# A hybrid decoder layer on one core: 45 matrix passes moved ahead of the first attention score, and a smaller allowance per attention step

## The chip, the core and the metric

The kernel runs on one core of one Trainium2 chip. The core has a matrix engine (TensorE, PE in the rows, with its weight loads as PEld), a vector engine (VectorE, DVE), an activation engine (ScalarE, ACT), a general engine (GpSimd, POOL) and a queue engine that only issues transfers (SyncE, SP). Each engine works through its own list of instructions in order and waits on semaphores for the others. Sixteen DMA engines move data between the core's memory and the chip's main memory; most transfers are issued by SP, some by ACT. The metric is the device time of one execution in microseconds, as the median of three runs.

## The reference

One decoder layer over 1024 tokens of width 1024, in float32:

- a root-mean-square norm and one projection of 3592 columns, split between two groups of heads;
- group one: four heads of a gated delta rule, with short convolutions on q, k and v, in chunks, and a gated norm;
- group two: four heads of differential attention. A head has two query/key maps of 64 columns. Each map gives causal scores with a relative-position bias and a softmax; the second map, times a learned lambda, is taken from the first, and the result is multiplied with the values and normed;
- the outputs of both groups side by side through one output projection, added to the input;
- a norm, a gated feed-forward layer of 2816 columns, added, and a last norm.

The lines of the reference that the change lies on:

```
s = jnp.einsum('bqhmd,bkhmd->bhmqk', q_blk, k).astype(jnp.float32)
s = s + bias.transpose(2, 0, 1)[None, :, None]
s = jnp.where(rel >= 0, s, -jnp.inf)
p = jax.nn.softmax(s, axis=-1)
p = p[:, :, 0] - lam * p[:, :, 1]
return jnp.einsum('bhqk,bkhe->bqhe', p.astype(v.dtype), v)
```

## The kernel before, in words

Dense products are computed to float32 accuracy from operands split into a high and a low part: `mm3` (lines 143 to 146) issues three passes, high by high, high by low and low by high. A **pass** below is one such matmul instruction with 512 moving columns.

The program runs in this order: norm and transposition of the input (`xT_h`, `xT_l`); values of all attention heads; the delta-rule heads; queries and keys of attention heads 0 and 1; then the **attention part**, into which other matrix work is woven; then the feed-forward layer.

The attention part has 32 **steps** k (list `steps`): four heads, eight blocks of 128 queries each, blocks 0 to 7 for heads 0 to 2 and 7 to 0 for head 3. Block i sees i+1 blocks of keys. A step's work is spread over the loop: `emit_S(k)` computes the scores of both maps, adds the bias, takes the maximum (DVE) and the exponential (ACT); `emit_P(k)` forms the difference of the two maps (DVE, line 931); `emit_T(k-1)` transposes the step before (line 946); `emit_PV(k-2)` multiplies the one before that with the values (line 961).

The other matrix work, the **filler**, is the generator `fill` (line 785). In this order it yields: queries of head 2 (48 passes, called Q2 below), keys of head 2 (K2), Q3, K3, with the gating of a delta-rule head (`finish_gate`) between or inside them; four empty yields (`SKIP`); 16 units of 12 passes of the output projection's first half (tiles named `fl<-w_h,av`); a wait until blocks 7 to 4 of head 3 are through; and 8 more units of 12 passes. In K2 the gating of head 0 stands between the first 24 passes and the last 24 (the call `mid()`): it transposes into the two `fl` buffers that the passes also use, and DVE (line 745) reads them together with a tile `cv<-sz` that SP loads. That load needs a buffer that holds Q2 until Q2 has been written to main memory.

`pump(n)` takes n passes from the filler; what a call takes too much is owed by the next. `share(k)` sets n for a step by the block number i: 22 - 5i/2, of which 5 come after the transposes, 4 between two groups of transposes in long steps, and the rest before; where that rest is negative it is nothing, so a long step gets 9. Over a head these are 22, 19.5, 17, 14.5, 12, 9.5, 9 and 9 passes. With them, K3's last pass falls into step 12 and the output projection's last into step 29.

SP's list is kept in the order of the program (`manual_schedule`). The other engines' lists are ordered by a scheduler that goes by its own durations. `load_head(h)` (line 698) loads a head's queries, keys (`ak<-ks`) and bias, `load_v` its values; both are called at steps 4, 12 and 20 for the next head, and before the loop for head 0. The keys of a head are written to main memory by ACT's queue (lines 604 and 605) and loaded again from there. After K3, `fetch_o` loads quarters of the output weights (`w_raw<-in_w_out`) into the space that K3's operands leave, and `take_o` splits them (ACT line 151, then DVE line 153 or POOL line 157). Each unit adds to a residual tile `xh` (SP line 775, DVE line 770).

Of the kernel before, what the change touches and what calls it, by code (L numbers as in the profile page):

```python
# [31 lines left out]
SQRT_MAX = 1.8446743e19  # L32
LAM_CAP = 1e12
SKIP = 4
LAM_INIT = 0.8 - 0.6


# [31 lines left out]
def decoder_kernel(ctx: ExitStack, tc: tile.TileContext, a: dict, out: bass.AP):  # L69
# [100 lines left out]
    def cvt(dtype=F32):  # L170
        return cv.tile([P, T], dtype, name="cv", bufs=4)
# [75 lines left out]
    nc.sync.dma_start(out=dnw, in_=a["diff_norm_w"][0].rearrange("(p o) -> p o", o=1))  # L247
    nc.vector.tensor_scalar(out=dnw, in0=dnw, scalar1=1.0 - LAM_INIT, scalar2=None, op0=ALU.mult)

    ab = const.tile([P, NT, 8], F32, name="ab")  # L250
    for half in range(2):
        n = 264 if half == 0 else 256
# [47 lines left out]
    for i, nm in enumerate(("lambda_q1", "lambda_k1", "lambda_q2", "lambda_k2")):  # L300
# [8 lines left out]
    nlam, mag, kap, nlc, epsi, thr = (lc[:, i:i + 1] for i in range(6))  # L309
    nc.vector.scalar_tensor_tensor(out=nlam, in0=ls[:, 1:2], scalar=-LAM_INIT, in1=ls[:, 0:1],  # L310
                                   op0=ALU.add, op1=ALU.subtract)
# [86 lines left out]
    def fetch(key, src, shape, which=0):  # L398
        pool, bufs = wpools[which]
        raw = pool.tile(shape, F32, name="w_raw", bufs=bufs)  # L400
        nc.sync.dma_start(out=raw, in_=src)
        raws[key] = pool, raw, shape
# [5 lines left out]
    def qk_col(h, is_q):  # L408
        c = (C_QD if is_q else C_KD) + h * P
        return w_in_v[:, :, c:c + P], [P, NK, P]  # L410
# [221 lines left out]
    for j in range(NT):  # L632
# [38 lines left out]
        for h in range(H):  # L671
            ps = pss[h]
            i = h * 8 + j
# [25 lines left out]
    def load_head(h):  # L699
        load_q(h, first_half(h))  # L700
        kt = ap_.tile([P, 2, T], F32R, name="ak", bufs=2)
        nc.sync.dma_start(out=kt.bitcast(F32), in_=ks_dr[h].rearrange("(m d) t -> d m t", m=2))
        kk = [kt[:, m, :] for m in range(2)]
        bias = ap_.tile([P, 256], F32, name="bias", bufs=2)
        nc.sync.dma_start(out=bias, in_=bias2_dr[:, h, :])
        head[h] = kk, bias

    def first_half(h):
        return 1 if h == H - 1 else 0
# [4 lines left out]
    def load_q(h, half):  # L714
        hc = slice(half * 512, (half + 1) * 512)
        parts = []
        for nm, src in (("aqh", qh_dr[h]), ("aql", ql_dr[h])):
            qt = ap_.tile([P, 2, 512], F32R, name=nm, bufs=2)
            for o in range(2):
                nc.sync.dma_start(out=qt[o * DH:(o + 1) * DH].bitcast(F32),  # L720
                                  in_=src[:, hc].rearrange("(m d) t -> d m t", m=2))
            parts.append(qt)
        queries[h, half] = parts

    def load_v(h):
        vals[h] = ap_.tile([P, NT, P], F32, name="avd", bufs=2)
        nc.sync.dma_start(out=vals[h], in_=vd_dr[h])
# [29 lines left out]
    def fetch_o(group, u, i):  # L757
        us = slice(u * 512, (u + 1) * 512)
        fetch((group, u, i), wo_v[:, 4 * group + 2 * i:4 * group + 2 * i + 2, us], [P, 2, 512], i)
# [24 lines left out]
    def fill():  # L784
# [25 lines left out]
        fetch_o(1, 0, 1)  # L810
        for _ in range(SKIP):
            yield -1
# [39 lines left out]
    def load_mix_d(half, n):  # L852
        for h in range(n):
            hc = slice(half * 512, (half + 1) * 512)
            m = late["mix"][half][h]
            raw = m[:, 512:1024].bitcast(F32)
            nc.sync.dma_start(out=raw, in_=md[h][:, hc])
            nc.scalar.copy(out=m[:, 0:512], in_=raw)
            nc.gpsimd.tensor_tensor(out=m[:, 512:1024], in0=raw, in1=m[:, 0:512].bitcast(F32), op=ALU.subtract)
# [3 lines left out]
    def share(k):  # L863
        i = steps[k][1] if k < len(steps) else 0
        prev = steps[k - 1][1] if 0 < k <= len(steps) else 0
        n = 22 - 5 * i / 2
        pb = 4 if prev >= 4 else 0
        return max(0, n - pb - 5), pb, 5

# [3 lines left out]
    def pump(n):  # L873
        nonlocal credit
        credit += n
        while credit > 0:
            c = next(filler, -1)
            if c < 0:
                credit = 0
                return  # L880
            credit -= c
# [53 lines left out]
    def emit_T(k, gap):  # L935
        h, i = steps[k]
        pp, rz = st[k]
        pt = ap_.tile([P, T], F32, name="apt", bufs=2)
        for b in range((i + 4) // 4):
            if b:  # L940
                pump(gap)
            ps = sma()
            nblk = min(4, i + 1 - 4 * b)
            for kk in range(nblk):
                kb = 4 * b + kk
                nc.tensor.transpose(ps[:, kk * P:(kk + 1) * P], pp[:, kb * P:(kb + 1) * P], ident)
            nc.scalar.copy(out=pt[:, b * 512:b * 512 + nblk * P], in_=ps[:, :nblk * P])
        st[k] = pt, rz
# [3 lines left out]
    def emit_PV(k):  # L952
        h, i = steps[k]
        pt, rz = st.pop(k)
        vd = vals[h]
        if k % 4 == 0:
            osum[h] = sma(), ap_.tile([P, 512], F32, name="aon", bufs=2)
        O, on = osum[h]
        oc = slice((i % 4) * P, (i % 4 + 1) * P)
        for kb in range(i + 1):  # L960
            nc.tensor.matmul(O[:, oc], lhsT=pt[:, kb * P:(kb + 1) * P], rhs=vd[:, kb, :],  # L961
                             start=(kb == 0), stop=(kb == i))
        nc.scalar.activation(out=on[:, oc], in_=O[:, oc], func=AF.Copy, scale=rz[:, 0:1])
        if k % 4 != 3:
            return
        nc.scalar.activation(out=O, in_=on, func=AF.Square)
        ms = small.tile([P, 4], F32, name="ams", bufs=3)
        nc.vector.tensor_reduce(out=ms, in_=O.rearrange("p (a b) -> p a b", a=4), axis=AX.X, op=ALU.add)
        ok = small.tile([P, 4], F32, name="aok", bufs=3)
        nc.vector.tensor_scalar(out=ok, in0=ms, scalar1=thr, scalar2=None, op0=ALU.is_lt)  # L970
        nc.vector.tensor_scalar(out=ms, in0=ms, scalar1=1.0 / DV, scalar2=epsi, op0=ALU.mult, op1=ALU.add)
        nc.vector.tensor_scalar(out=ms, in0=ms, scalar1=1e-37, scalar2=None, op0=ALU.max)
        nc.gpsimd.tensor_tensor(out=ms, in0=ms, in1=epow_neg[:, 0:4], op=ALU.pow)
        nc.vector.tensor_tensor(out=ms, in0=ms, in1=ok, op=ALU.mult)
        onv = on.rearrange("p (a b) -> p a b", a=4)
        nc.vector.tensor_tensor(out=onv, in0=onv,
                                in1=ms.rearrange("p (a o) -> p a o", o=1).broadcast_to([P, 4, P]), op=ALU.mult)
        osum["on"] = on
# [22 lines left out]
    with tc.manual_schedule(engines={mybir.EngineType.SP}):  # L1001
        fetch((2, True), *qk_col(2, True))
        fetch((2, False), *qk_col(2, False))
        load_head(0)
        load_v(0)
        for k in range(len(steps) + 4):

            def values():
                if 2 <= k < len(steps) + 2:
                    emit_PV(k - 2)  # L1010

            if k < len(steps):
                emit_S(k, values)
                if k % NT == 0:
                    load_q(k // NT, 1 - first_half(k // NT))
                if k % NT == 4 and k // NT + 1 < H:
                    load_head(k // NT + 1)
                    load_v(k // NT + 1)
            else:
                values()  # L1020
            if k == 28:
                late["mix"][1] = [cvt(F32R) for h in range(H)]
                load_mix_d(1, H - 1)
            pa, pb, pc = share(k)
            pump(pa)
            if 1 <= k <= len(steps):
                emit_T(k - 1, pb)
            pump(pc)
            if k > 2 and (k - 3) % 4 == 3:
                emit_OT(k - 3)  # L1030
            if k < len(steps):
                emit_P(k)
            if k == len(steps):
                while 0 not in late["mix"]:
                    pump(12)
                load_mix_d(0, H - 1)
        while "d1" in late:
            c = next(filler, None)
            if c is None:
                break  # L1040
# [369 lines left out]
```

## Time and profile before

| | |
|---|---|
| median of 3 runs | 1378.44 us (1376.91 to 1378.69) |
| the profiled execution | 1377.38 us |
| its span, first to last instruction | 1375.5 us |
| mean granted share of TensorE's clock | 0.988 |
| attention part in that span | about 406 to 657 us |
| PE busy, share of the span | 95% |
| DVE, ACT, POOL busy | 56%, 36%, 19% |

The span is divided into stages that bind differently, so shares over the whole span say little about one stage. Times in the rows are counted from the first instruction. Matmuls are pipelined: one pass is shown as 0.39 us long, while passes that follow each other start 0.23 us apart. Idle time of an engine stands in square brackets with what ended it.

### The profile page before, as it was taken

To read this page: it belongs to the slowest core of one execution; us is meant where nothing else is said; L and a number is where in the kernel's file an instruction comes from. 1 tells how busy PE (TensorE), PEld (TensorE's weight loads), DVE (VectorE), ACT (ScalarE), POOL (GpSimd) and SP (SyncE) were. 2 spreads that over 40 slices of the span, in tenths; PEclk is the share of its full clock that TensorE was granted. 3 is DMA by queue.
4 is the path that set the end of the run, shared out by engine and by line. 5 is a ranking of instruction groups with operands and counts; after the bars stand their busy time and mean duration, and the time that the engine had idled before them with its cause. 6 is when DMAs were issued, how large, how long until landed. Compare 5 with 4: busy or idle time off the path is not lost.

```text
span 1375.5 us, 17042 instructions
## 1 busy us (share of the span) xinstructions
PE 1305.1 (95%) x6540; PEld 1086.2 (79%) x6540; DVE 768.1 (56%) x1282; ACT 497.1 (36%) x948; POOL 262.5 (19%) x211
## 2 busy tenths in 40 slices
PE   6999999899988998998889999999999999999997
PEld 6968888798967777887667877787878788788886
DVE  6516649625833675876884555455545536545325
ACT  5233321233733654553543333232323235112104
POOL 1010052100042331113332121211121214200003
PEclk9999999999998999999999999999999999999999
DMA  7321113101055655734432233222222248422003
GB/s 216 110 62 47 31 44 97 29 1 47 1 145 182 208 179 185 237 119 168 145 100 77 94 100 98 79 75 92 92 77 73 80 134 280 152 92 92 0 1 123
DMA packets 122425, 143.31 MB, mean 104 GB/s; under 512 B 13632, under 2 KB 90728, under 8 KB 122344
## 3 DMA queue, kind: packets, MB, share of 16 engines
q1 hardware_dynamic: 114432, 128.07, 30.0%
q10 hardware_dynamic: 7912, 14.16, 2.8%
q8 instruction: 51, 0.84, 0.3%
q14 instruction: 30, 0.25, 0.1%
HBM read 103.40 MB, written 38.80 MB: 103 GB/s over the span
## 4 chain that ended last, share of the span: by engine, by line
PE 70%; DVE 13%; DMA 5%; issue 4%; ACT 4%; POOL 3%; SPq 1%; POOLq 0%; DVEq 0%; ACTq 0%
PE big L1177 17%; PE sm L1177 8%; PE fl L144 4%; PE fl L145 4%; PE fl L146 4%; PE fl L1177 4%; PE big L144 3%; PE big L145 3%; PE big L146 3%; PE sm L144 3%; PE sm L146 3%; PE sm L145 3%; PE sm L961 1%; DVE tmp L509 1%; DMA ks<-cv 1%
## 5 line engine op out<-in xcount | busy, mean ns | idle before, releaser
L144 PE MATMUL big<-xT_h,w_h 128*128 128x512 f32 x320 | 127.8, 399 | 0.7 <-DVE cv L435 0.7
L146 PE MATMUL big<-xT_h,w_l 128*128 128x512 f32 x320 | 126.9, 397 | 0.5 <-DVE w_l L153 0.5
L145 PE MATMUL big<-xT_l,w_h 128*128 128x512 f32 x320 | 126.2, 394 | 0.0
L1190 DVE TENSOR_TENSOR av<-big,av 128x512 f32<-128x512 f32 x88 | 60.5, 689 | 109.3 <-PE big L1177 109.2
L157 POOL TENSOR_TENSOR w_l<-w_raw,w_h 128x512 fp32r<-128x512 f32 x36 | 49.0, 1384 | 244.0 <-ACT w_h L151 244.0
L1177 PE MATMUL big<-hT_h,cv 128*128 128x512 f32 x264 | 90.8, 405 | 2.4 <-DVE av L1190 2.4
L1177 PE MATMUL big<-hT_h,avl 128*128 128x512 f32 x264 | 89.2, 399 | 1.1 <-DVE av L1190 1.1
L151 ACT CAST w_h<-w_raw 128x1024 fp32r<-128x1024 f32 x32 | 33.5, 1051 | 110.5 <-PE big L145 94.7
L144 PEld LDWEIGHTS big<-xT_h,w_h 128*128 128x128 f32 x320 | 60.7, 190 | 13.9 <-issue 2.2
L146 PEld LDWEIGHTS big<-xT_h,w_l 128*128 128x128 f32 x320 | 60.5, 189 | 13.2 <-DVE w_l L153 0.9
L145 PEld LDWEIGHTS big<-xT_l,w_h 128*128 128x128 f32 x320 | 60.6, 189 | 12.1 <-issue 0.2
L1177 PEld LDWEIGHTS big<-hT_h,cv 128*128 128x128 f32 x264 | 50.4, 191 | 20.2 <-DVE av L1190 9.8
L1177 PEld LDWEIGHTS big<-hT_h,avl 128*128 128x128 f32 x264 | 49.5, 188 | 18.1 <-DVE av L1190 8.0
L1177 PE MATMUL sm<-hB_h,avl 128*128 128x512 f32 x176 | 58.8, 395 | 1.1 <-ACT hB_h L1107 1.1
L1082 POOL TENSOR_TENSOR avl<-xh,avl 128x512 fp32r<-128x512 f32 x23 | 30.8, 1338 | 148.2 <-ACT avl L1081 148.2
L1190 DVE TENSOR_TENSOR x<-fl,x 128x512 f32<-128x512 f32 x48 | 33.0, 687 | 45.6 <-PE fl L146 45.6
L1190 DVE TENSOR_TENSOR x<-sm,x 128x512 f32<-128x512 f32 x48 | 33.0, 687 | 44.8 <-PE sm L146 44.1
L1177 PE MATMUL sm<-hB_h,cv 128*128 128x512 f32 x176 | 57.9, 389 | 0.0
L919 ACT ACTIVATE ae<-big,mx 128x128 f32<-128x128 f32 (+7 forms) x64 | 47.3, 741 | 27.7 <-DVE mx L910 11.6
L1082 POOL TENSOR_TENSOR cv<-xh,cv 128x512 fp32r<-128x512 f32 x22 | 28.3, 1288 | 146.3 <-ACT cv L1081 146.3
L1145 DVE TENSOR_TENSOR xh<-w_raw 128x512 f32<-128x512 f32 x45 | 31.0, 689 | 45.1 <-DMA w_raw<-in_w_gate_up 45.1
L435 DVE SCALAR_TENSOR_TENSOR cv<-big,convw,cv 128x1023 f32<-128x1023 f32 (+2 forms) x36 | 46.0, 1278 | 15.0 <-ACT cv L433 14.4
(431 smaller groups left out, 3532.1 us busy)
## 6 DMA issues: line engine op xcount, KB each, us to landing
w_raw<-in_w_gate_up SPq DMA_DIRECT2D x44, 512.0 KB, 4.0
w_raw<-in_w_in SPq DMA_DIRECT2D x24, 512.0 KB, 4.0
act<-av SPq DMA_DIRECT2D x22, 512.0 KB, 2.6
w_raw<-act SPq DMA_DIRECT2D x22, 512.0 KB, 4.2
cv<-in_w_down SPq DMA_DIRECT2D x20, 512.0 KB, 4.4
xt<-in_x SPq DMA_DIRECT2D x8, 512.0 KB, 5.5
ks<-cv ACTq DMA_DIRECT2D x8, 512.0 KB, 12.5
aqh<-qh SPq DMA_DIRECT2D x16, 256.0 KB, 5.2
```

Source lines behind the costliest of these rows:

```text
L144: nc.tensor.matmul(ps, lhsT=lh, rhs=rh, start=start, stop=False)
L145: nc.tensor.matmul(ps, lhsT=lh, rhs=rl, start=False, stop=False)
L146: nc.tensor.matmul(ps, lhsT=ll, rhs=rh, start=False, stop=stop)
L151: nc.scalar.copy(out=h, in_=raw)
L157: eng.tensor_tensor(out=l[:, c], in0=raw[:, c], in1=h[:, c].bitcast(F32), op=ALU.subtract)
L435: nc.vector.scalar_tensor_tensor(out=acc[:, d:], in0=ps[:, :T - d], scalar=convw[:, ct, 3 - d:4 - d], in1=acc[:, d:], op0=ALU.mult, op1=AL ...
L509: nc.vector.tensor_tensor(out=tv, in0=B[:, i + 1:, i:i + 1].broadcast_to([P, nr, ncol]), in1=X[:, i:i + 1, :ncol].broadcast_to([P, nr, nco ...
L919: nc.scalar.activation(out=e[:, :n].rearrange("p (b c) -> p b c", b=nb), in_=s[:, :, :w], func=AF.Exp, bias=mx[:, m:m + 1], accum_out=zs[: ...
L1082: eng.tensor_tensor(out=l, in0=raw, in1=h.bitcast(F32), op=ALU.subtract)
L1145: nc.vector.tensor_tensor(out=r, in0=a0, in1=a1, op=alu)
L1177: nc.tensor.matmul(ps, lhsT=x[:, k, :], rhs=y[:, k, :], start=begin and k == 0 and n == 0, stop=k == HALF - 1 and n == 2, skip_group_check ...
L1190: nc.vector.tensor_tensor(out=out, in0=in0, in1=in1, op=ALU.add)
```

## The change

The filler now gives 45 passes before the first score, and each step's allowance is 1.25 passes lower.

```diff
@@ -32,6 +32,7 @@
 SKIP = 4
+FIRST = 45
 LAM_INIT = 0.8 - 0.6
@@ -863,7 +864,7 @@
     def share(k):
         i = steps[k][1] if k < len(steps) else 0
         prev = steps[k - 1][1] if 0 < k <= len(steps) else 0
-        n = 22 - 5 * i / 2
+        n = 20.75 - 5 * i / 2
         pb = 4 if prev >= 4 else 0
         return max(0, n - pb - 5), pb, 5
@@ -1009,6 +1010,8 @@
+            if k == 0:
+                pump(FIRST)
             if k < len(steps):
                 emit_S(k, values)
```

Over a head the allowances are now 20.75, 18.25, 15.75, 13.25, 10.75, 9, 9 and 9: 105.75 instead of 112.5, so 27 fewer over the four heads against 45 given first. K3's last pass moves from step 12 to step 10, the output projection's last from step 29 to step 28. In the changed kernel's lists, line numbers are one higher up to line 1010 and three higher behind it.

PE, from the end of head 1's projections to the first score. `big` with 512 columns are passes of head 1's queries and keys, `fl` are passes of Q2, and the rows with `ak` are the first scores. Before:

```order
L146 MATMUL big<-xT_h,w_l 128x512
L144 MATMUL fl<-xT_h,w_h 128x512
L904 MATMUL big<-ak,aqh 128x128
L905 MATMUL big<-ak,aql 128x128
L904 MATMUL big<-ak,aqh 128x128
L905 MATMUL big<-ak,aql 128x128
L145 MATMUL fl<-xT_l,w_h 128x512
```

Now (the pieces at the first `fl` pass, at the first `big` pass behind them, and at the scores):

```order
L145 MATMUL fl<-xT_h,w_h 128x512
L146 MATMUL fl<-xT_l,w_h 128x512
...
L145 MATMUL fl<-xT_h,w_h 128x512
L145 MATMUL big<-xT_h,w_h 128x512
L146 MATMUL big<-xT_l,w_h 128x512
...
L147 MATMUL fl<-xT_h,w_l 128x512
L905 MATMUL big<-ak,aqh 128x128
L906 MATMUL big<-ak,aql 128x128
```

Before, one `fl` pass stands ahead of the first score, and the 24 passes of the second half of head 1's keys stand behind it. Now 10 `fl` passes, those 24, and 35 more `fl` passes stand ahead of it.

ACT, at the first exponential (`ae`). `cv<-big` is the copy of head 1's keys out of the accumulators, `w_h_3692` the high part of Q3's weights, `cv_3437` belongs to Q2. Before:

```order
L596 ACTIVATE cv_3352<-big_3344 128x512
L597 CAST cv_3351<-cv_3352 128x512
L919 ACT_TABLE_LOAD
L919 ACTIVATE ae_3436,z_3431<-big_3433,mx_3432 128x128
```

Now:

```order
L605 DMA ks1_72<-cv_3351 2x64x1024
L606 DMA ks1_72<-cv_3352 128x1024
L597 ACTIVATE cv_3437<-fl_3438 128x512
L598 CAST cv_3436<-cv_3437 128x512
L152 CAST w_h_3692<-w_raw_3516 128x1024
L920 ACT_TABLE_LOAD
L920 ACTIVATE ae_3494,z_3489<-big_3491,mx_3490 128x128
```

The write of head 1's keys (`ks1`), a copy of Q2 and the cast of Q3's weights have come ahead of the first exponentials.

SP, around the load of head 2 (`qh2`, `ql2`, `ks2` are its queries and keys, `in_x` the residual rows). Before:

```order
L720 DMA aqh_4214<-qh2_65 64x2x512
L702 DMA ak_4220<-ks2_73 128x2x1024
L727 DMA avd_4224<-vd_dr_75 128x1024
L401 DMA w_raw_4304<-in_w_out 128x2x512
L401 DMA w_raw_4331<-in_w_out 128x2x512
L775 DMA xh_4425<-in_x 128x512
```

Now:

```order
L402 DMA w_raw_4172<-in_w_out 128x2x512
L402 DMA w_raw_4199<-in_w_out 128x2x512
L721 DMA aqh_4268<-qh2_65 64x2x512
L703 DMA ak_4274<-ks2_73 128x2x1024
L728 DMA avd_4278<-vd_dr_75 128x1024
L776 DMA xh_4280<-in_x 128x512
```

Of the five quarters of output weights that SP fetches after K3, the first and the last are shown. Before, head 2 is loaded ahead of them; now it stands behind the last of them, and the residual rows stand behind head 2.

## Rows read from the trace of the kernel before

**Rows 1.** The page, busy time of each engine over the span.

```profile
PE 1305.1 (95%) x6540; PEld 1086.2 (79%) x6540; DVE 768.1 (56%) x1282; ACT 497.1 (36%) x948; POOL 262.5 (19%) x211
```

**Rows 2.** Timeline of PE at the first score: start, length, what, idle before.

```profile
406.20 0.39 PE L146 MATMUL big<-xT_h,w_l 128*128 128x512 f32 x1
406.43 0.39 PE L144 MATMUL fl<-xT_h,w_h 128*128 128x512 f32 x1
417.24 0.45 PE L904 MATMUL big<-ak,aqh 128*128 128x128 f32 x1 [10.43 <-DMA ak<-ks]
...
419.09 0.63 PE L144 MATMUL fl<-xT_h,w_h 128*128 128x512 f32 x1
419.52 0.63 PE L145 MATMUL fl<-xT_l,w_h 128*128 128x512 f32 x1
```

**Rows 3.** The chain that ended last, 370 to 660: start, length, what.

```profile
394.73 13.25 DMA ks<-cv
408.04 9.11 DMA ak<-ks
...
450.50 1.40 DVE cv L745 x2
...
480.86 1.79 PE sm L961 x16
...
516.30 0.95 ACT w_h L151
...
518.52 7.71 DMA w_raw<-in_w_out
```

**Rows 4.** Timeline of ACT, 389 to 440.

```profile
410.28 0.60 ACT L596 ACTIVATE cv<-big 128x512 f32<-128x512 f32 x1 [5.30 <-DMA aqh<-qh]
...
420.37 1.28 ACT L919 ACT_TABLE_LOAD   x1 [8.84 <-DVE mx L915]
421.66 0.37 ACT L919 ACTIVATE ae<-big,mx 128x128 f32<-128x128 f32 x1
```

**Rows 5.** Stretches of 2 us: busy time by engine, granted clock, DMA share, GB/s.

```profile
422.00:424.00 2.00, 2.00 (x10) 1.63 (x9) 0.74 (x3) 0.47 (x4) 0.00 (x0) 1.00 1.14 234
...
426.00:428.00 2.00, 2.00 (x11) 1.65 (x10) 0.00 (x0) 1.86 (x3) 0.76 (x1) 1.00 0.03 7
```

**Rows 6.** The same for 12 us at the first score.

```profile
406.00:418.00 12.00, 1.57 (x8) 1.14 (x6) 0.00 (x0) 1.21 (x2) 2.94 (x3) 0.70 0.78 257
```

**Rows 7.** Timeline of SP's queue, 375 to 640.

```profile
419.35 0.39 SPq L401 DMA_DIRECT2D w_raw<-in_w_in  x1
444.10 0.33 SPq L739 DMA_DIRECT2D cv<-sz  x1
...
519.45 10.82 SPq L401 DMA_DIRECT2D w_raw<-in_w_out  x2
530.31 0.95 SPq L775 DMA_DIRECT2D xh<-in_x  x2
```

**Rows 8.** The tile sz: issue to landing of its transfers.

```profile
DMA to landing us min/median/max: 2.6/4.6/9.7
```

**Rows 9.** DMA issues, 440 to 451: engine, count, size, median us to landing.

```profile
ql<-cv ACTq DMA_DIRECT2D x1, 512.0 KB, 3.1
```

**Rows 10.** DMA issues, 554 to 560.

```profile
ak<-ks SPq DMA_DIRECT2D x1, 1024.0 KB, 9.3
```

**Rows 11.** Timeline of PE at K2's second half.

```profile
451.30 0.49 PE L144 MATMUL fl<-xT_h,w_h 128*128 128x512 f32 x1
```

**Rows 12.** Timeline of PE from K3's last pass to the third unit behind it.

```profile
509.50 0.40 PE L146 MATMUL fl<-xT_h,w_l 128*128 128x512 f32 x1
...
528.72 0.39 PE L904 MATMUL big<-ak,aqh 128*128 128x256 f32 x1 [3.68 <-ACT ae L919]
...
535.35 0.50 PE L144 MATMUL fl<-w_h,av 128*128 128x512 f32 x1 [1.00 <-DVE xh L770]
```

**Rows 13.** Timeline of PE near the end of the attention part.

```profile
625.38 0.53 PE L946 MATMUL sm<-ident,ae 128*128 128x128 f32 x3 [3.83 <-DVE ae L931]
```

## The prediction

> **What bounds the kernel now.** I read the page's busy times first. PE is busy for 95% of the span [rows 1], so a change that only reorders matmuls can win no more than idle time of PE, and time in which PE ran slowly. Next I read PE's timeline at the place of the change. Before the first score PE stands still for 10.43 us, the longest pause of the attention part, and the row says what ended it: the load of head 0's keys [rows 2]. The chain shows why: the keys' write took 13.25 us to land, and their load, which can only start then, 9.11 us more [rows 3]. Nothing shortens that here. The pause is empty only because the score stands in front of Q2's passes in PE's list. After it the passes start 0.43 us apart (419.09, 419.52) instead of 0.23 (406.20, 406.43) [rows 2], and the granted clock over 406 to 418 averages 0.70 [rows 6]: part of that stretch was at 1.2 GHz instead of 2.4. Last I read the two places where the filler itself waits, since the change brings the filler there sooner: the gating inside K2 (PE goes on at 451.30 [rows 11], once DVE's line 745, begun at 450.50, has freed the accumulators [rows 3]), and the seam behind K3, where PE waits 3.68 and 1.00 us [rows 12].
>
> **The change part by part.** No instruction is added or removed; every term is idle time that goes or comes.
>
> *The pause at the first score.* The 10 passes that now come first take PE from 406.43 to 408.7 (10 x 0.23). The 24 passes behind them write the second half of a tile whose first half ACT copies out from 410.28 to 410.88 [rows 4], a copy that the change doesn't move; so 2.2 us of the pause stay and 10.43 - 2.2 = 8.2 go. With so short a pause I take the clock to stay up: six passes at 0.43 instead of 0.23 are 1.2 us, the four scores among them about 0.4. Gain: 8.2 + 1.6 = 9.8 us. The score itself now starts at about 410.9 + 59 x 0.23 = 424.4 instead of 417.24, 7 us later. What hides that is filler: 21 passes stand behind it.
>
> *The gating inside K2.* Its cover shrinks, because attention is later and the filler earlier. Before, PE did the scores of steps 4 and 5, the transposes of steps 2 and 3 and their products with the values before the second half of K2. In the new list only half of step 4's scores stands ahead. The rest is 7 transposes and 14 passes with the values at 0.11 us (16 such take 1.79 [rows 3]), and 11 score passes which I put at 0.15 to 0.17 by their columns against 0.23 for 512: 4.1 us, about 4.5 with the switches between them. So without a wait PE would reach that place at 451.30 - 9.8 - 4.5 = 437.0. When does the wait end? ACT now has the cast of Q3's weights ahead of the first exponentials. Those weights are issued at 419.35 [rows 7] and have landed by 426, since the DMA share is down to 0.03 then [rows 5]. But the write of head 1's keys (1 MB) now falls into this burst, which moves 234 GB/s [rows 5]: up to 4.5 us more. I take 428. Then: cast 1.0, table load 1.28, two exponentials about 0.8, copy 0.60, cast 0.62 [rows 4] make 4.3; Q2's write about 3.1 [rows 9]; the load of sz 4.6 [rows 8]; line 745 0.7. Sum: 440.7. Loss: 440.7 - 437.0 = 3.7. Bounds: weights at 426 give 1.7; weights at 430.5, and 6.4 us from sz's issue to line 745 as before (444.10 to 450.50 [rows 7, 3]), give 8.
>
> By the Trainium skill (DMA: Bandwidth & Descriptors, section "Issuing engines are not separate DMA queues") transfers issued by different engines end up on the same 16 DMA engines and interleave. That speaks against the change, for the key write on ACT's queue then takes its whole share from SP's loads: by the rule alone the weights land at 430.5 and the loss is 6.2; by the row alone, with the write hidden, it is 1.7.
>
> *The seam behind K3.* Before, 25.45 us lie between K3's end (509.90) and the third unit (535.35) [rows 12]: five quarters of weights load, split and free each other's buffers (cast from 516.30, the next load 518.52, landed 7.71 later [rows 3]), SP comes free at 530.27 and then fetches the residual rows [rows 7]. Now the load of head 2 stands on SP between the last quarter and those rows. Queued behind it: head 2's own first scores, for its keys take 9.3 us [rows 10], and the third unit. In return the first cast no longer stands behind two exponentials on ACT, which I count as 2.5 us. SP is then free 17.9 us after K3's end, the keys are issued 2.9 us later and land at 30, the residual rows by 31.5, and PE goes on at 32. In these 32 us PE has more to do than it had in 25.45: by its list 7 more transposes, 18 more passes with the values (0.11 each) and some 1.6 us of scores, 4.6 us with the switches. Loss: 32 - 25.45 - 4.6, about 2. With some passes behind the longer pause at the lower clock I take 2.5. Bounds: rows landed by 29 give a gain of 1; without the 2.5 us, and the rows 1.1 us later still, it is a loss of 5.5.
>
> *The allowance.* Steps with blocks 5 to 7 get 9 passes as before (one 9.5); the short steps lose 1.25 of 12 to 22. PE had hardly a pause in those, so I count nothing; without that cover the price is the seam's. At the end the filler runs dry one step sooner, at a place that already has a wait of 3.83 us [rows 13]. There the last weights' casts move ahead of the attention's work, which can shorten that wait, while the empty step can lengthen it: 0, from -2 to +2.
>
> *Sum.* 9.8 - 3.7 - 2.5 - 0 = 3.6 us off the profiled execution's 1377.38 us, that is 1373.8. That execution lies 1.06 us below the median of the runs shown, so I predict 1374.8. Bounds: 9.8 - 1.7 + 1 + 2 = 11.1 off (1367), and 9.8 - 8 - 5.5 - 2 = 5.7 on (1384).
>
> **The rivals.** *The pause only moves (no change).* Weights at 430.5 make the loss inside K2 6.2, and the seam loses 3.5: 9.8 - 9.7, 1378.3. For it: SP's queue and the DMA engines are the same before and after, and both waits are chains of transfers (13.25, 9.11, 7.71 us [rows 3]) that more filler doesn't shorten. Against it: the DMA share of 0.03 at 426 leaves room for a write.
>
> *Head 2 comes too late (slower).* One mechanism, on SP: head 2's load waits until the last quarter's buffer is free. If that is 20.4 us after K3's end as before (530.27 - 509.90), the keys land at 32.6, the rows at 35 and PE resumes at 36: the seam loses 36 - 25.45 - 4.6 = 6, and with a lower clock behind a pause of 10 us some 7. With 6 lost inside K2 that is 9.8 - 13 = 3.2 slower, 1381.6. It decides once PE resumes later than some 33 us after K3's end with the first loss at its upper end, or 36 with it at 3.7. For it: in the old list the head's load was out long before, and now nothing else stands there to be done. Against it: the last cast's place on ACT.
>
> *Nearly all of the pause is kept.* The key write is hidden and the residual rows come early: 9.8 - 1.7 + 1, or 1369. For it: the row at 426. Against it: the longer queue on SP.
>
> That the passes don't stand where the change says is ruled out by PE's list: 69 passes are ahead of the first score.
>
> **How the numbers follow.** Forecast, 1372 to 1375.5: 0.33. Nearly all kept, 1367 to 1372: 0.15. No change, 1375.7 to 1381.2: 0.30. Slower, above that: 0.22. A measurement of this kernel can tell about 0.2%, 2.8 us, from no change; so faster has 0.33 + 0.15 = 0.48, same 0.30, slower 0.22. The range leaves out one in ten on either side: from 1368.5, inside the third rival, to 1382.5, beyond the middle of the slower one. Faster and slower both hold chances, so the forecast's own range stands above.
>
> **What would show it.** Right: the pause before the first score falls to about 2 us, and 69 passes 0.23 us apart end at some 424; the first exponential starts near 430; PE waits 3 to 5 us in front of K2's second half, which starts near 441; between K3's end and the third unit some 32 us, with one long pause that the load of head 2's keys ends. The forecast is wrong if K2's second half starts later than 444, if the third unit starts over 35 us behind K3's end, or if a new wait over 2 us appears in the short steps.

## The result and the profile after

The changed kernel takes 1387.31 us (median of 4 runs, 1386.42 to 1390.26) against 1378.57 us before: a ratio of 1.0072, 95% interval 1.0059 to 1.0085. It is slower by about 9 us; 1374.8 had been forecast, with a range that ended at 1382.5. A second set of runs gave 1.0054 (1.0035 to 1.0072). The profiled execution has a span of 1384.6 us against 1375.5.

All of it arose in the attention part. From the first `fl` pass to the first transposes of the next stage PE runs the same 1222 matmuls before and now. They took 251.36 us (406.43 to 657.79) and take 261.79 us (404.22 to 666.01): 10.4 us more. What lies ahead of them was 2.2 us shorter in this execution and what follows 0.9 us longer. The stretch before, then now (length, busy time of PE, PEld, DVE, ACT and POOL, granted clock, DMA share, GB/s):

```profile
406.43:657.79 251.36, 222.52 (x1222) 186.15 (x1220) 161.43 (x294) 128.46 (x287) 68.57 (x56) 0.97 0.58 183
```

```profile
404.22:666.01 261.79, 227.78 (x1222) 189.42 (x1220) 154.43 (x294) 128.35 (x287) 66.43 (x56) 0.94 0.56 175
```

So about half of the loss is standing still (34.0 us instead of 28.8), and half is slower running (227.78 us instead of 222.52, at a granted clock of 0.94 instead of 0.97).

First, PE's timeline from the first `fl` pass on, which answers to [rows 2]. Columns: start, length, what, idle before with what ended it.

```profile
404.22 0.39 PE L145 MATMUL fl<-xT_h,w_h 128*128 128x512 f32 x1
...
408.77 0.50 PE L145 MATMUL big<-xT_h,w_h 128*128 128x512 f32 x1 [2.13 <-ACT cv L597]
...
422.07 0.39 PE L147 MATMUL fl<-xT_h,w_l 128*128 128x512 f32 x1
422.30 0.22 PE L905 MATMUL big<-ak,aqh 128*128 128x128 f32 x1
...
438.60 1.12 PE L745 MATMUL fl<-ident,av 128*128 128x128 f32 x4 [9.05 <-ACT cv L597]
...
442.07 0.80 PE L905 MATMUL big<-ak,aqh 128*128 128x512 f32 x1 [0.87 <-ACT ae L920]
...
448.50 0.76 PE L145 MATMUL fl<-xT_h,w_h 128*128 128x512 f32 x1 [1.18 <-DVE cv L746]
```

The pause of 10.43 us is gone and 2.13 are left. But from 429.55 on PE stands for 9.05 us in front of the gating's transposes, which need an accumulator that ACT has yet to copy out. ACT's own list says why it had not.

```profile
416.57 0.51 ACTq L605 DMA_DIRECT2D ks<-cv  x1
...
420.30 0.62 ACT L598 CAST cv<-cv 128x512 fp32r<-128x512 f32 x1
434.89 1.04 ACT L152 CAST w_h<-w_raw 128x1024 fp32r<-128x1024 f32 x1 [13.98 <-DMA w_raw<-in_w_in]
...
437.25 0.37 ACT L920 ACTIVATE ae<-big,mx 128x128 f32<-128x128 f32 x1
...
437.95 0.59 ACT L597 ACTIVATE cv<-fl 128x512 f32<-128x512 f32 x1
```

ACT waits 13.98 us for Q3's weights, and the exponentials and the copy (437.95) are queued behind that cast. The chain that ended last, with start and length, names the transfers on it:

```profile
392.55 13.24 DMA ks<-cv
...
406.28 10.71 DMA bias<-bias_dr
417.06 17.76 DMA w_raw<-in_w_in
...
458.13 12.66 DMA ks<-cv
...
514.16 3.82 DMA w_raw<-in_w_out
...
520.34 8.84 DMA w_raw<-in_w_out
```

The 512 KB of Q3's weights took 17.76 us. Up to 424 us the DMA engines were full with several transfers; from 424 to 434 us they were nearly idle, and the weights had still not landed:

```profile
416.00:424.00 8.00, 8.00 (x39) 6.70 (x38) 0.86 (x2) 1.76 (x3) 4.55 (x4) 1.00 1.03 242
424.00:434.00 10.00, 5.54 (x27) 4.32 (x25) 0.00 (x0) 0.00 (x0) 0.00 (x0) 0.87 0.13 53
```

(Columns as above.) A share of 0.13 is what two engines of sixteen give when they are always busy. The DMA view of the last 10 us splits it by queue, with packets, MB and share:

```profile
q10 hardware_dynamic: 117, 0.47, 11.4%
q1 hardware_dynamic: 112, 0.06, 1.9%
```

0.47 MB in 117 packets are 4 KB each: rows of the key write, on ACT's queue. 0.06 MB in 112 packets are about 512 bytes each: the weights, on SP's. The two counts are nearly equal, so I read it as the two queues taking turns, packet by packet, on two engines.

Three further waits have no counterpart of their size before. One is behind head 2's key write, in ACT's list and in PE's:

```profile
464.48 0.60 ACT L597 ACTIVATE cv<-fl 128x512 f32<-128x512 f32 x1
470.87 0.62 ACT L598 CAST cv<-cv 128x512 fp32r<-128x512 f32 x1 [5.80 <-DMA ks<-cv]
...
471.79 0.60 ACT L967 ACTIVATE sm<-aon 128x512 f32<-128x512 f32 x1
```

```profile
473.17 0.47 PE L947 MATMUL sm<-ident,ae 128*128 128x128 f32 x1 [4.61 <-DVE ams L969]
```

One stands before the first score of step 12 (head 1, block 4), where PE needs an accumulator that the exponentials of an earlier step still read:

```profile
506.66 0.63 PE L905 MATMUL big<-ak,aqh 128*128 128x320 f32 x1 [2.78 <-ACT ae L920]
```

The third is in the seam behind K3 [rows 12]: ACT waits for the third quarter of the output weights (8.84 us in the chain, against 7.71 [rows 3]), the copy behind it is late, and PE stands. The third unit starts at 550.40, so the seam lasts 550.40 - (513.73 + 0.40) = 36.3 us against 25.45.

```profile
529.20 1.04 ACT L152 CAST w_h<-w_raw 128x1024 fp32r<-128x1024 f32 x1 [5.33 <-DMA w_raw<-in_w_out]
530.15 0.58 ACT L948 COPY apt<-sm 128x512 f32<-128x512 f32 x1
```

```profile
513.73 0.40 PE L147 MATMUL fl<-xT_h,w_l 128*128 128x512 f32 x1
...
530.78 2.08 PE L962 MATMUL sm<-avd,apt 128*128 128x128 f32 x8 [4.91 <-ACT apt L948]
...
550.40 0.50 PE L145 MATMUL fl<-w_h,av 128*128 128x512 f32 x1
```

Behind each of these waits PE runs at half speed for a while: its passes start 0.43 us apart. Two stretches, before and then now (the granted clock is the third number from the end):

```profile
430.00:452.00 22.00, 21.38 (x118) 18.06 (x117) 14.07 (x24) 13.12 (x33) 7.39 (x6) 1.00 0.58 177
...
468.00:500.00 32.00, 30.59 (x178) 25.64 (x178) 18.71 (x37) 19.64 (x46) 12.54 (x10) 1.00 0.52 165
```

```profile
430.00:452.00 22.00, 10.92 (x37) 8.71 (x38) 12.08 (x22) 11.89 (x29) 6.77 (x6) 0.61 0.57 176
...
468.00:500.00 32.00, 27.39 (x156) 23.76 (x155) 18.26 (x33) 17.36 (x37) 6.08 (x5) 0.89 0.37 114
```

At the end, where 3.83 us were lost [rows 13], 0.68 are:

```profile
637.51 0.55 PE L947 MATMUL sm<-ident,ae 128*128 128x128 f32 x3 [0.68 <-DVE ae L932]
```

### The profile page after: what moved, and what is told of

Its sections match the earlier page's. It is cut to its first block, busy times and chain, and to the rows that moved or that the text cites. A ratio compares the mean times of both kernels' runs of the same rounds, so it can differ in the third digit from the quotient of the medians.

```text
span 1384.6 us, 17039 instructions
## 1 busy us (share of the span) xinstructions
PE 1312.1 (95%) x6540; PEld 1090.5 (79%) x6540; DVE 760.6 (55%) x1282; ACT 496.9 (36%) x948; POOL 259.7 (19%) x211
## 4 chain that ended last, share of the span: by engine, by line
PE 67%; DVE 11%; DMA 10%; issue 4%; ACT 4%; POOL 2%; SPq 1%; POOLq 0%; DVEq 0%; ACTq 0%
PE big L1180 18%; PE sm L1180 8%; PE fl L1180 4%; PE fl L145 3%; PE big L145 3%; PE fl L147 3%; PE fl L146 3%; PE big L146 3%; PE big L147 3%; PE sm L145 2%; PE sm L147 2%; PE sm L146 2%; DMA ks<-cv 2%; DMA w_raw<-in_w_in 2%; DMA x<-xh 1%
```

## The experiments

**Theory A.** The first half of each key write (line 605 in the changed kernel) is a transfer of 2 x 64 rows. It moves over two DMA engines, for 10 us and more. Whatever else is in flight has its share on those two engines too and crawls with it, and what needs the written buffer waits. **Rival B:** the cast's place ahead of the exponentials is enough, whatever the load takes. **Rival C:** the lower allowance and head 2's load at the end of SP's queue, that is, the seam.

The table has all runs; "gating" is PE's wait in front of the gating's transposes (L745 or L744), "head 2" its wait behind head 2's key write (near 468), "seam" its longest behind K3, each from the one execution of the run that was profiled, in us. A dash: no such wait of 1.1 us or more; e6's 1.09 is given for comparison. Before had medians of 1379.0 (first four runs), 1380.57 (next four) and 1378.89 (last four).

| run | median us | ratio to before (95%) | gating | head 2 | seam |
|---|---|---|---|---|---|
| changed kernel | 1387.31 | 1.0072 (1.0059 to 1.0085) | 9.05 | 4.61 | 4.91 |
| e1_after_split | 1364.93 | 0.9897 (0.9873 to 0.9921) | - | - | - |
| e2_before_split | 1370.46 | 0.9926 (0.9898 to 0.9954) | - | - | - |
| e3_first_only | 1383.42 | 1.0018 (1.0000 to 1.0037) | 8.83 | 5.86 | 4.57 |
| e4_allow_only | 1381.38 | 1.0019 (1.0004 to 1.0034) | - | 1.32 | 5.58 |
| e5_split_head1 | 1380.91 | 1.0011 (0.9994 to 1.0027) | 1.56 | 4.65 | 4.73 |
| e6_after_head2 | 1391.19 | 1.0082 (1.0054 to 1.0109) | 1.09 | 6.51 | 4.32 |
| e7_split_head2 | 1370.63 | 0.9938 (0.9918 to 0.9958) | - | - | 2.51 |
| e8_split_first20 | 1365.40 | 0.9892 (0.9859 to 0.9925) | - | - | 1.98 |
| e9_weights_early | 1381.35 | 1.0016 (1.0002 to 1.0029) | 2.06 | 4.95 | 4.23 |
| e10_split_head2_keys | 1381.01 | 1.0013 (0.9999 to 1.0026) | 8.72 | - | 5.25 |
| e11_split_head3_keys | 1383.96 | 1.0027 (1.0000 to 1.0053) | 9.00 | 4.69 | 1.26 |
| e12_after_again | 1385.97 | 1.0054 (1.0035 to 1.0072) | 9.34 | 4.63 | 4.96 |

**e1 and e2: the slow half on all engines.** The same edit in the changed kernel and in the one before:

```diff
-            nc.scalar.dma_start(out=ks_dr[h].rearrange("(a d) t -> a d t", d=DH)[0::3], in_=sh.bitcast(F32))
+            for r, q in ((0, 0), (3, 1)): nc.scalar.dma_start(out=ks_dr[h][r * DH:(r + 1) * DH, :], in_=sh[q * DH:(q + 1) * DH].bitcast(F32))
```

> The changed kernel, but the half of the key write that goes out as 2 x 64 rows (line 605) is issued as two writes of 64 rows. Theory A (that half moves over two DMA engines for some 10 us, and the weights of Q3, issued at the same moment, have a share of their own behind it on those two): the write lands within 7 us of its issue instead of 13 to 18, Q3's weights within 7 us instead of 17.8, the 9.05 us in front of the gating's transposes and the 4.61 us at 468 go, and the low clock behind them: 1362 to 1370 us. Rival B (what costs is only that the cast stands ahead of the exponentials on ACT, with any length of the load): the wait shrinks by 2 us at most, 1383 to 1387. Rival C (the seam behind K3 with head 2's load at the end of the queue): 1382 to 1387, with the 4.91 us at the seam unchanged.

> The kernel before, with the same edit of the key write. Theory A: head 0's keys are written within 6 us instead of 13.25, so their load starts 7 us earlier; the pause of 10.43 us before the first score falls to 3 to 5 us, and the time to 1368 to 1373 us. Rival (the pause is bound by the 1 MB load and by the bandwidth of all transfers in it): the pause stays above 8 us, 1376 to 1379.

Measured: 22 us off the changed kernel, which is now faster than before by 1.0% (0.8 to 1.3%). The weights' load, issued at 411.13, landed in 8.6 us (within 7 had been expected), and the parts of head 1's write in about 3 (DMA issues from 411 and from 417 us: engine, count, KB, us to landing):

```profile
w_raw<-in_w_in SPq DMA_DIRECT2D x1, 512.0 KB, 8.6
...
ks<-cv ACTq DMA_DIRECT2D x2, 256.0 KB, 3.1
ks<-cv ACTq DMA_DIRECT2D x1, 512.0 KB, 2.6
```

PE reaches K2's second half 12.4 us earlier:

```profile
428.49 0.60 PE L745 MATMUL fl<-ident,av 128*128 128x128 f32 x4
...
436.08 0.50 PE L145 MATMUL fl<-xT_h,w_h 128*128 128x512 f32 x1 [1.18 <-DVE cv L746]
```

Rival B falls: the cast stands at the same place on ACT and costs PE nothing there. One thing besides the write differs: head 0's part lands sooner, so the load went out 6.1 us ahead of head 1's write (417.26), and e1 alone doesn't tell a short write from a changed order. e5 below does.

In the kernel before, the pause falls from 10.43 to 4.68 us and the time by 0.7% (0.5 to 1.0%); the 3.68 us of the seam fall to 0.80 as well. So the two-engine write had been at work in the old kernel too, and its own length was part of the pause.

```profile
412.16 0.44 PE L904 MATMUL big<-ak,aqh 128*128 128x128 f32 x1 [4.68 <-DMA ak<-ks]
```

**e3 and e4: the two parts of the change alone.** In e3 the allowance is 22 - 5i/2 again; in e4 FIRST is left out.

> Only the 45 passes ahead of the first score; the allowances as before (22 less 5i/2). Theory A: the order at the first score is that of the changed kernel, so the weights' load collides with the key write as there: a wait of 8 to 10 us in front of the gating's transposes, 1384 to 1390 us. Rival C (the lower allowance and what it does at the seam is the cause): 1372 to 1379.

> Only the lower allowances (20.75 less 5i/2), no passes ahead of the first score. Theory A: the pause of 10.4 us stays and nothing collides: 1376 to 1381 us, within 0.2% of before. Rival C: the shorter steps cost 6 us and more, 1384 or later.

Measured: about 0.2% each, both at the edge of what can be told from no change. e3 keeps all three waits of the table, as theory A has it, but comes out below the range that was expected, and its ten runs spread from 1377.44 to 1386.07. e4 has no wait at the gating and 1.32 us behind head 2's write, but 5.58 us at the seam, where head 3's key write (16.1 us to landing) and output weights (13.4 us) are in flight together. Neither part alone gives the loss. So the wait at the gating, and nearly all of the one behind head 2's write, come with the 45 passes. The wait of 2.78 us before step 12 needs both parts: at that score e3 and e4 have none (e3 at 513.70, e4 at 496.55), and e8, with less than half of both and split writes, has 1.12.

**e5, e10 and e11: one head's write at a time.** The edit of e1 for h == 1, 2 or 3 only.

> The changed kernel with only head 1's key write split into writes of 64 rows; the order on every engine is that of the changed kernel otherwise. Theory A: the 9.05 us in front of the gating's transposes go (Q3's weights land within 9 us of their issue), and the passes at half speed behind them, 12 us together; the waits that belong to the writes of heads 2 and 3 (4.61 us at 468, 4.91 us at 526) stay in some size: 1372 to 1378 us. If the fast writes of the other heads alone made the earlier gain: 1384 to 1388.

> The changed kernel with only head 2's key write split. Theory A: the copy of Q3's first half no longer waits 5.8 us on ACT for the write to free its buffer, the 4.61 us at 468 go, with the half-speed passes behind them: 5 to 8 us below the changed kernel of this call. If that wait belongs to something else: within 2 us of it.

> The changed kernel with only head 3's key write split; the order on every engine is that of the changed kernel otherwise. Theory A: the third and fourth quarter of the output weights no longer share two engines with that write (8.8 and 13.9 us to landing), so the 4.91 us at 526 and the half-speed passes behind them go: 4 to 7 us below the changed kernel of this call. Rival C (head 2's load behind the output weights is what the seam waits for): within 2 us of it.

> The changed kernel again, to have it on the same chip as the three edits of this call: 1384 to 1392 us, 0.5 to 0.9% above before.

Measured: each edit takes away most or all of its own wait and leaves the other two, as the table shows. e5 is the clean test of the collision: the write (418.91) still goes out just ahead of the load (419.60), as in the changed kernel, and the load takes 10.07 us instead of 17.76.

```profile
418.91 3.36 ACTq L605 DMA_DIRECT2D ks<-cv  x2
...
429.74 1.05 ACT L152 CAST w_h<-w_raw 128x1024 fp32r<-128x1024 f32 x1 [5.53 <-DMA w_raw<-in_w_in]
```

e5's ratio lies 0.4 to 0.6% below the changed kernel's two ratios, e10 5.0 us below e12 (5 to 8 expected), e11 2.0 us below it, less than expected and within the intervals. For e5, 1372 to 1378 had been expected; with weights that still took 10.07 us it kept 1.56 us in front of the gating and 2.02 at the next scores. In e11 the third quarter of the output weights took 5.73 us instead of 8.84 and the wait at the seam became 1.26 us. The third unit starts 545.17 - (512.34 + 0.39) = 32.4 us behind K3, not 36.3:

```profile
512.34 0.39 PE L147 MATMUL fl<-xT_h,w_l 128*128 128x512 f32 x1
...
526.46 1.16 PE L962 MATMUL sm<-avd,apt 128*128 128x128 f32 x8 [1.26 <-ACT apt L948]
...
545.17 0.50 PE L145 MATMUL fl<-w_h,av 128*128 128x512 f32 x1
```

**e9: the load out of the write's way.** No write is touched; Q3's weights are fetched earlier on SP.

```diff
             if k == 0:
                 pump(FIRST)
+                fetch((3, True), *qk_col(3, True))
...
-        fetch((3, True), *qk_col(3, True))
         finish_norm(1)
```

> The changed kernel with the load of Q3's weights four places earlier on SP, ahead of the second half of head 0's queries; no write is touched and the other engines' lists stay. Theory A (the load and the slow half of head 1's key write share two DMA engines): issued near 409 us, some 8 us ahead of the write, the weights have landed by 423; the wait in front of the gating's transposes falls from 9 to under 2 us, the rest stays: 1377 to 1382 us on the scale of before at 1378.6, 6 to 9 us below the changed kernel of this call. Rival (that much data is in flight in these 20 us, whatever the order): the wait moves to the queries or stays, within 3 us of the changed kernel.

Measured: 4.6 us below e12, less than the 6 to 9 expected. The load was issued at 410.56, 9.4 us ahead of the write (419.96), and ACT's cast waited for PE, not for the load. What is left at the gating is ACT's copy of K2 waiting 2.42 us for the buffer that the slow write still holds:

```profile
426.80 1.05 ACT L152 CAST w_h<-w_raw 128x1024 fp32r<-128x1024 f32 x1 [2.49 <-PE fl L146]
...
436.56 0.60 ACT L597 ACTIVATE cv<-fl 128x512 f32<-128x512 f32 x1 [2.42 <-DMA ks<-cv]
```

So both halves of theory A are seen apart: the load delayed, and the buffer held. The write itself came 1.5 us later here than in the changed kernel, counted from PE's restart (410.63 to 419.96 against 408.77 to 416.57), at a granted clock of 0.89, so not all of the distance is the edit's.

**e6 and e7: rival C.** Head 2 is loaded from step 9, ahead of the output weights, in the changed kernel and with the split writes.

```diff
-                if k % NT == 4 and k // NT + 1 < H:
+                if k in (4, 9, 20):
```

> The changed kernel with the load of head 2 called at step 9 instead of 12, so that it stands ahead of the output weights on SP. Theory A: the collision at head 1's write is untouched (a wait of about 9 us in front of the gating's transposes); the wait of 4.91 us at the seam belongs to head 3's key write against the output weights, so little changes: 1384 to 1390 us. Rival C (head 2's place in SP's queue is the cause of the loss): 1376 to 1381.

> The changed kernel with all key writes split and head 2 loaded from step 9. Theory A: with the writes short the seam has little left to win: within 3 us of the split alone (1362 to 1368). Rival C: the load's place still holds 5 us and more: 1360 or less.

Measured: no gain in e6, and e7 is slower than e1 by 0.4%. The load's late place is not the cause; the output weights behind it came late instead (in e7 PE waits 2.51 us for their low part and 2.00 for a residual row). One expectation failed: the wait at the gating was not 9 us in e6 but 1.09; where e6 lost what this saved is not shown. What differed there was the issue order. The weights were issued at 420.12 and the write at 421.42, 1.3 us behind; in the changed kernel the write (416.57) was 0.5 us ahead of the load (417.06). ACT's cast could start 11.65 us after the load's issue:

```profile
421.42 0.51 ACTq L605 DMA_DIRECT2D ks<-cv  x1
...
431.77 1.05 ACT L152 CAST w_h<-w_raw 128x1024 fp32r<-128x1024 f32 x1 [6.01 <-DMA w_raw<-in_w_in]
```

**e8: a smaller head start.** With the writes split, FIRST = 20 and n = 21.5 - 5i/2.

> All key writes split, 20 passes first instead of 45, allowances of 21.5 less 5i/2. Theory A: with the writes split the pause before the first score is 4.7 us without any passes ahead of it, so 20 passes (4.5 us) cover it and the exponentials start earlier: 1362 to 1368 us, the same as with 45 passes or 2 us better. If the 45 passes win by something else than the pause: 1367 to 1371.

Measured: 1365.40, no different from e1: with short writes 45 passes win nothing over 20 that could be told. Both beat the two kernels of this case.

## Why the prediction was wrong

**The pause: right.** Forecast: 2.2 us stay, passes 0.23 us apart, the score 18 us behind the first `fl` pass (424.4 - 406.43). Measured: 2.13, and 422.30 - 404.22 = 18.1.

**The gating inside K2: the step that failed.** The forecast counted the key write as 1 MB in a burst at 234 GB/s, "up to 4.5 us more", and had the weights land at 428, at the latest at 430.5, that is 8.6 to 11.2 us after their issue. It was 17.76. The write was priced in bytes, but half of it has only two engines, and there a load of 64 packets on each engine (512 KB in 512-byte packets over sixteen) waits for a 4 KB packet before every one of its own. An estimate from the rows: 117 + 112 packets on two engines in 10 us are 0.17 us for a pair, and 64 pairs 11 us; the other 7 us fall into the full stretch up to 424. Instead of 3.7 us the place lost 9.05 + 0.87 + 1.18 and some 1.6 more for eight passes at 0.43 us. For the clock behind this wait the sum had no term at all, only a gain of 1.6 us at the pause and 0.5 at the seam; over the whole part slower running cost 5.3 us net. K2's second half started at 448.50, where the forecast had named 444 as the limit. The old trace held the hint: 1 MB of keys needed 13.25 us to be written and 9.11 to be read [rows 3]. "Nothing shortens that here", said of these two, was wrong as well: with the write split the pause is 4.68 us without any filler ahead of it (e2). And the DMA share of 0.03 at 426 [rows 5], which the forecast took for room, was room only because head 1's write had not begun:

```profile
428.34 0.49 ACTq L604 DMA_DIRECT2D ks<-cv  x1
```

Before, the load had been issued 9.0 us ahead of it (419.35 [rows 7]). Taking the pause away brought the write forward beside the load.

The Trainium skill (DMA: Bandwidth & Descriptors, section "Why a DMA increments its semaphore by 16 and not by 1") says that a transfer uses the largest number of engines, up to 16, that divides the outermost dimension on both sides. By that, 2 x 64 rows get two; the trace agrees, with a share of 0.13. The rule of the Trainium skill that the forecast quoted, that transfers of different engines interleave on the same 16 DMA engines, pointed the right way; the sum made with it was too small.

**The allowance: wrong, and a wait without a term.** "Nothing" was counted for the short steps, and a wait over 2 us in one was named as a sign of being wrong. It is the 2.78 us before step 12. The lower allowance makes it only together with the 45 passes (e3, e4, e8), and no edit of a write moved it (2.79 in e1); the chain leads from the late exponentials to DVE's maximum (line 916, 504.43) and to POOL's lines 974 and 599 (503.15 and 501.56), but what puts those so late stays open. The 4.61 us at 468 are another matter. They lie between the transposes of step 5, whose allowance lost only half a pass, and e3 has 5.86 us there with the old allowances. Head 2's write, 12.66 us long, still holds a buffer that ACT's copy of Q3 needs; e10 takes that wait away and 5 us with it. The forecast had no term for this place.

**The seam: the size and the reason were wrong.** 36.3 us, where 32 were forecast and 35 named as the limit. The forecast saw PE wait for head 2's keys. PE waited for ACT, and ACT for the third quarter of the output weights, which met head 3's key write (e11). With that write split the seam is 32.4 us, close to the forecast's 32, but no long pause for head 2's keys ends it, so the forecast's reason isn't borne out by that. Of the rivals, "head 2 comes too late" came nearest in size, but its mechanism is refuted by e6 and e7.

**The end: outside its bounds.** 0, from -2 to +2, was forecast; 3.1 us of the wait went. The mechanism that the forecast named for a gain, earlier casts of the last weights, was not tested.

**The sum.** With all writes split the change seems to gain: 1364.93 against 1370.46, 5.5 us, though the two intervals overlap. That this is near the forecast's 3.6 is luck, for the pause to be won there is 4.68 us and not 10.43. What stays open: the three heads split singly give some 6 to 8, 5 and 2 us, all four together 22. Head 0's write alone was not tried; in e1 it also brings Q3's load ahead of head 1's write, and the lists of the other engines differ a little.

## What to carry to other kernels

A pause can be what keeps two transfers apart: before filling it, list every transfer that is then issued earlier, and what is in flight at that moment. Price a transfer by the number of engines that it uses, not by its bytes; a DMA share that stays near 2/16 while something waits is the sign to look for, and the outermost dimension is what to mend. Fetch early enough that a cast in front of other work never waits (e9); putting such casts behind the work that frees accumulators is the other way, which was not tried here.

## What was not expected of the hardware

Two transfers on the same two DMA engines seem to have taken turns by packet, not by byte: 117 packets of 4 KB against 112 of 512 bytes in 10 us. A start of the load 1.8 us earlier against the write (0.5 us behind it in the changed kernel, 1.3 us ahead in e6) went with 11.65 us at most to landing, instead of 17.76. The clock had a part in that: behind a pause of 2.19 us in e6 the granted clock over the next stretch was 0.89, so that the passes ahead of the write took 1.5 us longer. Behind one of 2.13 us in the changed kernel it was 1.00. In e12, the changed kernel again, it was 1.00 behind a pause of 2.19 us too, so the length of the pause doesn't decide it. The three stretches, e6, the changed kernel and e12:

```profile
406.00:422.00 16.00, 13.81 (x55) 10.95 (x54) 0.00 (x0) 3.40 (x6) 5.70 (x6) 0.89 0.81 244
```

```profile
404.00:420.00 16.00, 13.87 (x61) 11.18 (x60) 0.00 (x0) 3.71 (x6) 6.56 (x6) 1.00 0.87 250
```

```profile
406.00:422.00 16.00, 13.80 (x61) 11.12 (x60) 0.00 (x0) 3.96 (x6) 6.26 (x5) 1.00 0.87 252
```

So one profiled execution shows which waits are possible, not how often they come. This may be why e3 spread over 9 us; that was not tried.
